# Moving four of twelve weight-sum sets from the recurrence into the output projection

## The chip, the core and the metric

The kernel runs on one core of a Trainium2 chip. A core has a matrix engine (PE, with PEld for its weight loads), three engines for elementwise work (DVE is VectorE, ACT is ScalarE, POOL is GpSimd), a queue engine (SP) that issues transfers, and 16 DMA engines that carry all transfers. Each engine works through its own list of instructions in order and waits on semaphores of the others. The metric is the time of one execution in microseconds (us), lower is better; comparisons are made between medians.

## The reference

Two decoder layers on x of 1024 tokens by 1024 features, all in float32. Layer 0 mixes tokens with a gated linear recurrence (HGRN2), layer 1 with a convolution module. Each mixer is followed by a normalisation with a residual, then a squared-ReLU MLP with a hidden width of 4096, then another normalisation. Cut to what matters here:

```python
for i in range(DEPTH):                                    # two layers
    mix = hgrn2_mixer(x, ...) if i % 2 == 0 else conformer_conv_mixer(x, ...)
    x = layer_norm(DEEPNORM_ALPHA * x + mix, ln_mix_g[i], ln_mix_b[i])
    ff = jnp.square(jax.nn.relu(x @ ffn_w1[i])) @ ffn_w2[i]
    x = layer_norm(DEEPNORM_ALPHA * x + ff, ln_ffn_g[i], ln_ffn_b[i])

def hgrn2_mixer(h, w_in, lb, norm_g, w_out):
    q, fz, v, g = jnp.split(h @ w_in, 4, axis=-1)
    ...                                                   # chunkwise recurrence per head -> o, RMS norm, gate
    return o.astype(h.dtype) @ w_out
```

## The kernel before, in words

Every large product is done by a scheme of seven products in place of eight blocks (the "forms" 1 to 7), each in three passes over high and low halves of float32 numbers. A form of a weight is a block or a sum of blocks. For the second MLP weight, `w2`, the sums are not made on an engine but by the DMA engines, ahead of time: for each of 8 slices `c` of each of the 2 layers there is a **set**, a buffer `sum_w2...` of four 512 KB blocks in DRAM. `block_sums` makes a set with five transfers: two plain copies of two blocks each (L419, L420), one accumulating transfer that adds two blocks at once (L421, 1024 KB), and two accumulating transfers of one block (L423, 512 KB), each of which needs the one ahead of it. Accumulating transfers go out on POOL's queue. The sets are read far later, in the down products of the two MLPs.

Where the 16 sets are made: 12 in the recurrence, with copies and adds on POOL's queue; 2 in the first MLP's up products (L1478, with copies on SP); 2 in layer 1 (L1810). `to_sum` is the list of sets still to make, layer 0 first.

The stages that the change touches, in order of time:

- **The recurrence** (60 to 425 us of the trace). The main loop runs over `PAIRS` and the forms in `ORDER`, 84 products of 12 matmuls (`ps<-xf,fs`). Between the matmuls a hand-written order of ticks (`later`, `tick`) places the work of the 8 heads: the order of all five engines is fixed by the program, with no scheduler. Twice per head `settle` squares the attention output on ACT (L735), POOL makes one over the root (L736 and `power_m_half`, L518), and ACT scales the output by it (L741), for which PE waits with its transposes (`ps<-ident,o`). Every sixth product of the loop, `block_sums` places a set on POOL's queue, its parts 12 ticks apart. A tick fixes only the order on a queue: POOL issues a transfer as soon as it has come to it and the semaphores allow.
- **The output projection** (425 to 509 us). 16 *entries*, one per 128 tokens and half of the columns: 24 matmuls `ps<-w,oT` into one of six PSUM banks, then DVE adds the residual (`y<-y,ps`). At each second half of the columns (entries 3, 4, 6, 7, 9, 11, 13 and 15) follows a norm: statistics on DVE, the power on POOL (L518, `mv<-mv,nhalf`), two DVE passes (`y<-y,mv,ln_mix_g` needs no power, `y<-y,mv,ln_mix_b` does), a store (`kept<-y`), and PE transposes. Here the tile framework's scheduler sets the order of every engine by a simulated timeline.
- **The start of the up products** (from 509 us). `up.form` multiplies the transposed norms by the first forms of `w1q`, which come as `raw` loads on SP (L90, L135) and are split on ACT (L72) and DVE. `x1_late` (L1191) has four small POOL copies there.

Of the kernel before, what the change touches and what calls it, by code (L numbers as in the profile page):

```python
# [8 lines left out]
F32 = mybir.dt.float32  # L9
# [3 lines left out]
ALU = mybir.AluOpType  # L13
PSUM = bass.MemoryType.PSUM

P = 128
# [4 lines left out]
HT = 512  # L21
# [23 lines left out]
ORDER = (1, 2, 6, 5, 7, 3, 4)  # L45
# [66 lines left out]
class Forms(Slots):  # L112
# [12 lines left out]
    def add(self, x, y, out=None):  # L125
        out = self.sums() if out is None else out
        self.vector.tensor_tensor(out=out, in0=x, in1=y, op=ALU.add)
        return out
# [140 lines left out]
def body(ctx, tc, d, out):  # L269
    nc = tc.nc  # L270
    cst = ctx.enter_context(tc.tile_pool(name="cst", bufs=1))
    stat = ctx.enter_context(tc.tile_pool(name="stat", bufs=4))
    dram = ctx.enter_context(tc.tile_pool(name="dram", bufs=1, space=bass.MemoryType.DRAM))
# [55 lines left out]
    def acc():  # L329
        return rings["mm"]()  # L330
# [40 lines left out]
    order = ExitStack()  # L371
# [12 lines left out]
    def later(n, job):  # L384
        if n:
            waiting.append((ticks[0] + n, job))
        else:
            job()

    def tick(n=1):  # L390
        for _ in range(n):
            ticks[0] += 1
            for at, job in [w for w in waiting if w[0] <= ticks[0]]:
                waiting.remove((at, job))
                job()

    sums = {}

    def block_sums(name, layer, c, after=None, gap=0, adds=None):

        t = sums[name, layer, c] = dram.tile([4, P, 1024], F32, name=f"sum_{name}{layer}{c}")
        v, w = t.rearrange("a p n -> p a n"), d[name][layer, c].rearrange("a p n -> p a n")
        queue = nc.sync if after is not None else nc.gpsimd
        if adds is not None:

            def copies(rows, after):
                nc.sync.dma_start(out=t[0:4:2, rows.start, 0:1], in_=after)
                queue.dma_start(out=v[rows, 0:2], in_=w[rows, 0:4:2])
                queue.dma_start(out=v[rows, 2:4], in_=w[rows, 0:2])

            copies(slice(16, P), after)
            adds.append(lambda after: copies(slice(0, 16), after))
            adds.append(lambda after: nc.gpsimd.dma_start(out=v[:, 0:2], in_=w[:, 2:4], accum_op=ALU.add))
            for i in (2, 3):
                adds.append(lambda after, i=i: nc.gpsimd.dma_start(out=v[:, i], in_=v[:, i - 1], accum_op=ALU.add, max_dma_last_dim=4096))
            return
        if after is not None:
            nc.sync.dma_start(out=t[0:4:2, 0, 0:1], in_=after)
        queue.dma_start(out=v[:, 0:2], in_=w[:, 0:4:2])  # L419
        later(gap // 2, lambda: queue.dma_start(out=v[:, 2:4], in_=w[:, 0:2]))  # L420
        parts = [lambda: nc.gpsimd.dma_start(out=v[:, 0:2], in_=w[:, 2:4], accum_op=ALU.add)]  # L421
        for i in (2, 3):
            parts.append(lambda i=i: nc.gpsimd.dma_start(out=v[:, i], in_=v[:, i - 1], accum_op=ALU.add, max_dma_last_dim=4096))  # L423
        for i, part in enumerate(parts):
            later((i + 1) * gap, part)

    to_sum = [(*of, c) for of in (("w2", 0), ("w2", 1)) for c in range(NFC)]

# [72 lines left out]
    for k in range(4):  # L501
        c = slice((k % 2) * HT, (k % 2 + 1) * HT)
# [466 lines left out]
    def seam():  # L969
        plan = [  # L970
            (5, lambda: fetch(0, 0)), (15, lambda: split_w(0, 0, 136)), (17, lambda: split_w(0, 1, 144)), (19, lambda: split_w(0, 3, 120)),
            (21, lambda: split_w(0, 2, 152)), (13, lambda: heads_in(0, 0, 4, 32)), (19, lambda: heads_in(0, 4, 6, 32)),
            (24, lambda: split_heads(0, 0)), (26, lambda: split_heads(0, 2)), (29, lambda: split_heads(0, 4)),
            (16, lambda: bring(0)), (17, lambda: bring(1)), (27, lambda: last_in(H - 2, 0, sixth[0])), (36, lambda: last_in(H - 1, 0, lastly[0])),
            (21, lambda: heads_in(1, 0, 6, 64)), (38, lambda: split_heads(1, 0)), (41, lambda: split_heads(1, 2)), (44, lambda: split_heads(1, 4)),
            (25, lambda: fetch(1, 80)), (39, lambda: split_w(1, 0, 112)), (42, lambda: split_w(1, 1, 128)),
            (45, lambda: split_w(1, 2, 96)), (47, lambda: split_w(1, 3, 104)),
            (43, lambda: last_in(H - 2, 1, sixth[1])), (46, lambda: last_in(H - 1, 1, lastly[1])),
        ]
        for n, job in plan:  # L980
            later(n, job)
# [25 lines left out]
    for p, (kind, j) in enumerate(PAIRS):  # L1007
        st = {"banks": dict(turn_of)}
        turn_of = {"z": turn_of["a"], "a": turn_of["b"], "b": turn_of["z"]}
        pace[1] = 0.0 if p == 0 else 0.6 if p < 3 else 0.5  # L1010
        if kind == "g" and p < len(PAIRS) - 1:
            to_load += [(2 * j, 0), (2 * j + 1, 1), (2 * j, 1), (2 * j + 1, 0)]
        if p == len(PAIRS) - 1:
            seam()
        for i in ORDER:
            if kind == "q" and i == 2:
                while any(a[0] <= j - 3 for a in active) or recs and recs[0] <= j - 3:
                    tick()
                    step()
            pair_product(p, i, made.pop(0), st)  # L1020
            later(2, make_form)
            if (7 * p + ORDER.index(i)) % 6 == 1 and len(to_sum) > 4:
                block_sums(*to_sum.pop(0), gap=12)
        if kind == "q":
            later(4, lambda j=j: recs.append(j))
    early_out = ((0, 0), (1, 0), (2, 0))
# [9 lines left out]
    tick(100)  # L1036
    assert not waiting and not loaded and not to_load and not gates, (waiting, gates)
    order.close()
    oT = [o[0] for o in oT]


# [94 lines left out]
    y = [view(160 + 16 * h, (NTB, D), F32, "y") for h in range(2)][::-1]  # L1136
# [57 lines left out]
    def x1_block(half, t):  # L1194
# [8 lines left out]
        if t < NTB - 1:  # L1203
            bg.chores += [lambda: x1_first(t), lambda: x1_second(t)]

    for half in range(2):
        for t, n in early_out + ((0, 1), (1, 1), (3, 0), (2, 1), (3, 1)) if half == 0 else [(t, n) for t in range(NTB) for n in range(2)]:
            ps = acc()
            if half or (t, n) not in early_out:
                product(ps, wide(oT[half], t, ws[n]))  # L1210
            yv = y[half][:, t, n * HT : (n + 1) * HT]
            vector.scalar_tensor_tensor(out=yv, in0=yv, scalar=ALPHA, in1=ps, op0=ALU.mult, op1=ALU.add)
            if n == 1:
                if half == 1 and t == 0:
                    early[0].ahead(1)
                x1_block(half, t)
                if half == 0 and t:
                    bg.chore()
    for e in early[1:]:
        e.ahead(2)  # L1220


    def store(layer, c, i, q, src):
# [260 lines left out]
    y = [view(32 + 16 * h, (NTB, D), F32, "y") for h in range(2)]  # L1484
# [371 lines left out]
    y = [view(kb, (NTB, D), F32, "y") for kb in (88, 112)]  # L1856
# [103 lines left out]
```

## Time and profile before

| what | us |
|---|---|
| median of 3 runs | 2056.83 (2054.85 to 2059.17) |
| the profiled execution | 2057.16 |
| its span in the trace | 2055.4 |
| PE busy in the span | 2023.6 (98%) |
| PE idle in the span | 31.8 |
| POOL busy in the span | 396.3 (19%) |
| DMA packets of the accumulating and copying queue of POOL (q0) | 12.2% of 16 engines' span |

Times of rows count from the span's start. A row of a timeline gives the start, the duration, the engine, the line, the operation with its tiles, and in brackets how long the engine had been idle before it and what ended that idle time. A row of a waits view gives the total, the number of times and the longest. Line L204 stands for every DVE and PE instruction, since a helper records them; they are told apart by their tiles. `ps` is PSUM. POOL's transfers have a short busy time (the issue); the landing is given apart.

### The profile page before, as it was taken

Reading aid. Unit: us, or ns where it says so; the run is one execution under the profiler, and the core shown is the slowest. Engines: PE = TensorE matmul, PEld = TensorE weight load, DVE = VectorE, ACT = ScalarE, POOL = GpSimd, SP = SyncE. Lnnn points to the kernel's source line nnn. Section 1 sums busy time; section 2 is a strip of 40 time slices with the busy share of each in tenths; the row PEclk is TensorE's granted clock in tenths of the full one; section 3 lists DMA queues with packets and bytes.
Section 4 is the critical chain, followed back from the end, with each engine's and each line's share of the span. In section 5 each row is a group of like instructions: output and inputs, shape, how many; then the busy total and the mean of one; then the engine's idle time right before and its main releaser. Section 6 shows DMA issues by size and latency. Waiting matters only on the chain. (4 is left out here: it accounts for less than half of the span.)

```text
span 2055.4 us, 29649 instructions
## 1 busy us (share of the span) xinstructions
PE 2023.6 (98%) x11144; PEld 1669.0 (81%) x11144; DVE 1488.1 (72%) x1978; ACT 1094.5 (53%) x1725; POOL 396.3 (19%) x405
## 2 busy tenths in 40 slices
PE   8999999999999999999999999999999999999998
PEld 7888887888787888888888888888888878888886
DVE  8698888877856675665567897889589666754456
ACT  5456565631655556444443776498615555443343
POOL 0112232111101000000001798089110000100002
PEclk9999999999999999999999999999999999999999
DMA  4778999842679776989998744496759768995542
GB/s 187 221 201 229 265 254 269 248 183 85 192 268 295 281 282 225 394 329 329 338 335 299 298 185 184 180 351 247 276 216 337 231 225 303 391 292 195 195 154 103
DMA packets 183944, 517.55 MB, mean 252 GB/s; under 512 B 17912, under 2 KB 49784, under 8 KB 182776
## 3 DMA queue, kind: packets, MB, share of 16 engines
q1 hardware_dynamic: 168312, 456.93, 61.7%
q0 software_dynamic: 15488, 58.72, 12.2%
q8 instruction: 87, 1.43, 0.3%
q14 instruction: 57, 0.47, 0.1%
HBM read 380.85 MB, written 201.85 MB: 283 GB/s over the span
## 5 line engine op out<-in xcount | busy, mean ns | idle before, releaser
L204 PE MATMUL ps<-dw,dh 128*128 128x512 f32 x2688 | 611.3, 389 | 0.5 <-DVE dh L204 0.5
L204 PEld LDWEIGHTS ps<-dw,dh 128*128 128x128 f32 x2688 | 504.3, 188 | 105.3 <-DVE dh L204 0.9
L204 PE MATMUL ps<-x1f,fw 128*128 128x512 f32 x1344 | 307.5, 390 | 5.2 <-ACT c L1266 2.3
L204 PEld LDWEIGHTS ps<-x1f,fw 128*128 128x128 f32 x1344 | 251.5, 188 | 59.7 <-issue 2.5
L204 PE MATMUL ps<-xf,fs 128*128 128x512 f32 x1008 | 248.6, 397 | 3.6 <-issue 1.7
L204 POOL TENSOR_TENSOR cb<-cb,prod 128x512 f32<-128x512 f32 x168 | 223.2, 1337 | 13.0 <-ACT prod L1591 2.4
L204 PEld LDWEIGHTS ps<-xf,fs 128*128 128x128 f32 x1008 | 184.0, 188 | 42.6 <-issue 1.9
L204 DVE TENSOR_TENSOR dh<-dh 128x1024 fp32r<-128x1024 f32 x112 | 136.5, 1222 | 109.4 <-ACT dh L72 109.3
L204 DVE SCALAR_TENSOR_TENSOR ps<-u,par,ps 128x512 f32<-128x512 f32 x296 | 206.0, 750 | 10.6 <-ACT ps L1603 9.3
L204 PE MATMUL ps<-xa,wa 128*128 128x512 f32 x864 | 203.3, 392 | 0.2
L72 ACT CAST dh<-dh 128x1024 fp32r<-128x1024 f32 x112 | 117.5, 1051 | 143.9 <-DMA dh<-hf 137.7
L72 ACT CAST dw<-dr 128x1024 fp32r<-128x1024 f32 x112 | 117.4, 1054 | 140.9 <-PE ps L204 125.5
L204 DVE TENSOR_TENSOR dw<-dr,dw 128x1024 fp32r<-128x1024 f32 x112 | 136.3, 1223 | 76.6 <-ACT dw L72 75.8
L204 PEld LDWEIGHTS ps<-xa,wa 128*128 128x128 f32 x864 | 160.3, 188 | 33.6 <-DMA wa<-ready 0.6
L1591 ACT ACTIVATE prod<-u,par 128x512 f32<-128x512 f32 x168 | 119.4, 726 | 34.2 <-POOL cb L204 33.5
L518 POOL TENSOR_TENSOR mv<-mv,nhalf 128x1 f32<-128x1 f32 x32 | 42.2, 1321 | 405.1 <-DVE mv L204 394.8
L204 PE MATMUL ps<-w,oT 128*128 128x512 f32 x384 | 89.9, 392 | 1.3 <-ACT oT L932 0.8
L204 PE MATMUL ps<-xb,wa 128*128 128x512 f32 x384 | 91.1, 393 | 0.0
L204 PE MATMUL ps<-vw,xf 128*128 128x512 f32 x336 | 79.9, 400 | 5.6 <-ACT vw L435 5.3
L204 PEld LDWEIGHTS ps<-w,oT 128*128 128x128 f32 x384 | 71.4, 188 | 16.6 <-ACT oT L932 1.2
L204 PEld LDWEIGHTS ps<-xb,wa 128*128 128x128 f32 x384 | 71.1, 188 | 14.3
L204 PEld LDWEIGHTS ps<-vw,xf 128*128 128x128 f32 x336 | 65.0, 194 | 20.1 <-ACT vw L435 5.3
(250 smaller groups left out, 2891.9 us busy)
## 6 DMA issues: line engine op xcount, KB each, us to landing
wa<-ready SPq DMA_DIRECT2D x140, 512.0 KB, 5.0
dh<-hf SPq DMA_DIRECT2D x112, 512.0 KB, 5.3
sum_w<-in_w_dram POOLq DMA_DIRECT2D x40, 1024.0 KB, 10.0
ready<-spare SPq DMA_DIRECT2D x76, 512.0 KB, 5.7
raw<-in_w1q_dram SPq DMA_DIRECT2D x66, 512.0 KB, 4.3
dr<-sum_w SPq DMA_DIRECT2D x64, 512.0 KB, 5.5
hf<-ht SPq DMA_DIRECT2D x112, 256.0 KB, 4.9
dr<-in_w_dram SPq DMA_DIRECT2D x48, 512.0 KB, 5.3
```

What stands on the lines that cost most here:

```text
L72: self.nc.scalar.copy(out=slot[:, 0, c], in_=raw[:, c])
L204: return op(*args, **kw)
L518: nc.gpsimd.tensor_tensor(out=dst, in0=src, in1=nhalf[:, :n], op=ALU.pow)
L1591: nc.scalar.activation(tp, u[:, k : k + HT], AF.Copy, scale=tap(j, k))
```

## The change

In the recurrence 8 sets are made in place of 12, one every ninth product, their parts 18 ticks apart. Four sets (of layer 1) move to the output projection. There, POOL's order is now written by hand, and no longer chosen by the scheduler: a table `turns` says behind which entry which part of which of the four sets is placed, so that each add stands on POOL's queue behind the power of that entry's norm. The two copies of these sets go out on SP, behind a small transfer of four numbers of `y` into the set's buffer, which holds them back until that entry's `y` is there. The sets in the first MLP and in layer 1 stay as they are.

```diff
@@ new helper @@
+    def sum_parts(name, layer, c):
+        t = sums[name, layer, c] = dram.tile([4, P, 1024], F32, name=f"sum_{name}{layer}{c}")
+        v, w = t.rearrange("a p n -> p a n"), d[name][layer, c].rearrange("a p n -> p a n")
+
+        def copies(after):
+            nc.sync.dma_start(out=t[0:4:2, 0, 0:1], in_=after)
+            nc.sync.dma_start(out=v[:, 0:2], in_=w[:, 0:4:2])
+            nc.sync.dma_start(out=v[:, 2:4], in_=w[:, 0:2])
+
+        def add(out, x, **kw):
+            return lambda after: nc.gpsimd.dma_start(out=out, in_=x, accum_op=ALU.add, **kw)
+
+        return [copies, add(v[:, 0:2], w[:, 2:4])] + [add(v[:, i], v[:, i - 1], max_dma_last_dim=4096) for i in (2, 3)]
@@ recurrence @@
-            if (7 * p + ORDER.index(i)) % 6 == 1 and len(to_sum) > 4:
-                block_sums(*to_sum.pop(0), gap=12)
+            if (7 * p + ORDER.index(i)) % 9 == 1 and len(to_sum) > 8:
+                block_sums(*to_sum.pop(0), gap=18)
...
     order.close()
+    order.enter_context(tc.manual_schedule(engines={mybir.EngineType.Pool}))
@@ output projection @@
+    parts, entry = [sum_parts(*to_sum.pop(0)) for _ in range(4)], 0
+    turns = {0: (0,), 3: (1,), 4: (0,), 6: (0, 1, 2), 8: (3,), 9: (0, 1, 2), 11: (1, 2, 3), 13: (2, 3), 15: (3,)}
     for half in range(2):
...
+            for k in turns.get(entry, ()):
+                parts[k].pop(0)(y[half][:2, t, n * HT : n * HT + 1])
+            entry += 1
+    assert not any(parts)
     for e in early[1:]:
         e.ahead(2)
+    order.close()
```

How the lists of instructions move, at the three places that the prediction speaks of. POOL's list around the two `settle` steps of the fourth head in the recurrence (`ss<-ss` is the mean, `ss<-ss,nhalf` the power; `sum_w` with a number is one set), before:

```order
L419 DMA sum_w_2457<-in_w_dram 128x2x1024
L420 DMA sum_w_2457<-in_w_dram 128x2x1024
L736 TENSOR_SCALAR ss<-ss 128x4
L518 TENSOR_TENSOR ss<-ss,nhalf 128x4
L423 DMA sum_w_2229<-sum_w_2229 128x1024
L421 DMA sum_w_2457<-in_w_dram 128x2x1024
L736 TENSOR_SCALAR ss<-ss 128x4
L518 TENSOR_TENSOR ss<-ss,nhalf 128x4
L423 DMA sum_w_2457<-sum_w_2457 128x1024
```

and with the change, at the same two steps:

```order
L420 DMA sum_w_2217<-in_w_dram 128x2x1024
L423 DMA sum_w_1816<-sum_w_1816 128x1024
L421 DMA sum_w_2217<-in_w_dram 128x2x1024
L751 TENSOR_SCALAR ss<-ss 128x4
L533 TENSOR_TENSOR ss<-ss,nhalf 128x4
L423 DMA sum_w_2217<-sum_w_2217 128x1024
L419 DMA sum_w_2541<-in_w_dram 128x2x1024
L751 TENSOR_SCALAR ss<-ss 128x4
L533 TENSOR_TENSOR ss<-ss,nhalf 128x4
L420 DMA sum_w_2541<-in_w_dram 128x2x1024
```

Between the two steps stood an add that needs two copies just issued (L421); now there stand the add of an older transfer and a copy that needs nothing.

POOL's list in the output projection had the eight powers in one row, with the copies of `x1_late` behind them:

```order
L736 TENSOR_SCALAR ss<-ss 128x4
L518 TENSOR_TENSOR ss<-ss,nhalf 128x4
L518 TENSOR_TENSOR mv<-mv,nhalf 128x1 x8
L1191 CAST x1f_4506<-fw 128x1 x2
L1191 CAST x1f_4510<-fw 128x1 x2
```

and has with the change, from the third power to the last but one (the sets are 4491 to 4494):

```order
L533 TENSOR_TENSOR mv<-mv,nhalf 128x1
L438 DMA sum_w_4491<-sum_w_4491 128x1024
L438 DMA sum_w_4492<-in_w_dram 128x2x1024
L533 TENSOR_TENSOR mv<-mv,nhalf 128x1 x2
L438 DMA sum_w_4491<-sum_w_4491 128x1024
L438 DMA sum_w_4492<-sum_w_4492 128x1024
L438 DMA sum_w_4493<-in_w_dram 128x2x1024
L533 TENSOR_TENSOR mv<-mv,nhalf 128x1
L438 DMA sum_w_4492<-sum_w_4492 128x1024
L438 DMA sum_w_4493<-sum_w_4493 128x1024
L438 DMA sum_w_4494<-in_w_dram 128x2x1024
L533 TENSOR_TENSOR mv<-mv,nhalf 128x1
```

Twelve adds now stand between and behind the powers; each waits on POOL's queue for the copy or add that it needs, with the next power behind it.

POOL's list around the two settles of the sixth head, before:

```order
L419 DMA sum_w_3242<-in_w_dram 128x2x1024
L420 DMA sum_w_3242<-in_w_dram 128x2x1024
L423 DMA sum_w_2921<-sum_w_2921 128x1024
L421 DMA sum_w_3242<-in_w_dram 128x2x1024
L736 TENSOR_SCALAR ss<-ss 128x4
L518 TENSOR_TENSOR ss<-ss,nhalf 128x4
L736 TENSOR_SCALAR ss<-ss 128x4
L518 TENSOR_TENSOR ss<-ss,nhalf 128x4
L423 DMA sum_w_3242<-sum_w_3242 128x1024
```

and with the change:

```order
L421 DMA sum_w_2903<-in_w_dram 128x2x1024
L423 DMA sum_w_2903<-sum_w_2903 128x1024
L419 DMA sum_w_3307<-in_w_dram 128x2x1024
L751 TENSOR_SCALAR ss<-ss 128x4
L533 TENSOR_TENSOR ss<-ss,nhalf 128x4
L420 DMA sum_w_3307<-in_w_dram 128x2x1024
L751 TENSOR_SCALAR ss<-ss 128x4
L533 TENSOR_TENSOR ss<-ss,nhalf 128x4
L423 DMA sum_w_2903<-sum_w_2903 128x1024
```

One copy stands ahead of the first settle there now, in place of two copies and two adds, and one between the two.

On SP's list in the output projection the small transfer and the two copies of a set stand behind the gain vectors' load (first set), the first, the third and the fourth store `kept<-y`; of the weight loads of the up products one stands between the third set's small transfer and its copies, and all others behind the fourth set's copies. The scheduler also moved a few DVE instructions of entries 8 to 11 past each other.

## The prediction

> **What bounds the kernel now.** First the page's busy times and the busy time by stage (stage, then busy time and count of each engine, granted clock, share of the DMA engines, GB/s):
>
> ```profile
> PE 2023.6 (98%) x11144; PEld 1669.0 (81%) x11144; DVE 1488.1 (72%) x1978; ACT 1094.5 (53%) x1725; POOL 396.3 (19%) x405
> 60.00:425.00 365.00, 356.18 (x3677) 294.44 (x3676) 293.67 (x471) 219.27 (x502) 79.42 (x94) 1.00 0.90 252
> 425.00:509.00 84.00, 84.00 (x398) 69.99 (x397) 64.34 (x95) 14.31 (x22) 10.44 (x7) 1.00 0.24 84
> 509.00:560.00 51.00, 47.69 (x214) 38.30 (x213) 46.18 (x54) 30.93 (x43) 8.66 (x9) 1.00 0.61 185
> ```
>
> PE sets the time: it idles 31.8 us in all. The recurrence (60 to 425) holds 365 - 356.18 = 8.8 of them, the output projection (425 to 509) none, the start of the up products 3.3. The DMA engines are 90% taken in the recurrence and 24% in the projection, and the change carries work from the one to the other. It can win at most the 8.8 us in which PE waits, so I read next what PE waits for there, and who made that late (total, times, longest):
>
> ```profile
> PE ps L204 <- issue: 1.7, 1, 1.7
> PE ps L204 <- DVE state L204: 1.4, 2, 0.9
> PE ps L204 <- ACT t L837: 1.2, 2, 0.9
> PE ps L204 <- ACT o L741: 1.1, 2, 0.7
> ...
> PE ps L204 <- DMA f<-vd: 0.2, 1, 0.2
> ```
>
> Only 0.2 us is a transfer directly. The others wait for ACT or DVE, so I followed the stalls back through the timelines. Two go back to the sets. At 268 POOL is late (POOL, ACT and PE in one stretch):
>
> ```profile
> 262.26 0.23 ACT L735 ACTIVATION_READ_ACCUMULATOR o<-ps 128x1 f32 x1
> 263.26 1.22 POOL L421 DMA_DIRECT2D sum_w<-in_w_dram  x1 [3.68 <-issue]
> 264.56 0.72 POOL L736 TENSOR_SCALAR ss<-ss 128x4 f32<-128x4 f32 x1
> 266.76 1.15 ACT L741 ACTIVATE o<-ps,ss 128x128 f32<-128x128 f32 x4 [1.94 <-POOL ss L518]
> 267.96 0.66 PE L204 MATMUL ps<-ident,o 128*128 128x128 f32 x4 [0.71 <-ACT o L741]
> ```
>
> ACT had its sums at 262.49. POOL stood until 263.26 at the add L421, which needs two copies just issued, and began the mean at 264.56: 2.07 us late, of which PE loses 0.71. At 343 ACT is late, since a store has not landed and its buffer isn't free:
>
> ```profile
> 342.37 0.59 ACT L837 COPY t<-ps 128x512 f32<-128x512 f32 x1 [1.72 <-DMA zd<-t]
> 343.00 2.09 PE L204 MATMUL ps<-xf,fs 128*128 128x512 f32 x8 [0.31 <-ACT t L837]
> 346.81 1.09 PE L204 MATMUL ps<-xf,fs 128*128 128x512 f32 x4 [1.71 <-issue]
> ```
>
> ACT loses 1.72, and PE 0.31 + 1.71 = 2.02 behind it. The other 8.8 - 0.71 - 2.02 - 0.2 = 5.9 us stand behind DVE and ACT, which work there without a transfer in sight: DVE is busy 293.67 of 365 us.
>
> **The change, part by part.** The load first (the recurrence's queues and transfers; KB each, then the median us to landing):
>
> ```profile
> q0 software_dynamic: 13248, 50.34, 56.6%
> sum_w<-in_w_dram POOLq DMA_DIRECT2D x36, 1024.0 KB, 10.0
> sum_w<-sum_w POOLq DMA_DIRECT2D x24, 512.0 KB, 7.1
> ```
>
> POOL's queue takes 0.566 x 365 = 207 us of all 16 engines for 12 sets, 17 us a set. Four sets less leave 365 x 0.90 - 69 = 260 us, a share of 0.71.
>
> *Recurrence, the wait at 268.* In the new order of POOL nothing that was just issued stands between the two settles of a head, only an add whose source has been in flight since before the first settle, and a copy. Gain 0.71; none, if another settle is caught instead. I take 0.7.
>
> *Recurrence, the wait at 343.* It lies at the sixth head's settles. Ahead of them POOL had issued a copy pair, a small add and a large add; now it has one copy there, behind an add whose source is long in flight, so the store has less beside it. Gain between 0 and 2.0; I take 1.5, nearer the whole, since ACT needs only 1.72 us less. The 5.9 us behind DVE and ACT stay: no instruction of theirs goes. The 20 issues of four sets leave POOL's list, which was not the bound.
>
> *Projection, POOL.* Here adds stand ahead of powers. The rows that tell what a late power costs:
>
> ```profile
> 452.85 1.28 DVE L204 SCALAR_TENSOR_TENSOR y<-y,mv,ln_mix_b 128x1024 f32<-128x1024 f32 x1 [0.45 <-POOL mv L518]
> 463.62 1.51 POOL L518 TENSOR_TENSOR mv<-mv,nhalf 128x1 f32<-128x1 f32 x1 [4.82 <-DVE mv L204]
> 465.17 1.29 DVE L204 SCALAR_TENSOR_TENSOR y<-y,mv,ln_mix_b 128x1024 f32<-128x1024 f32 x1 [0.44 <-POOL mv L518]
> 473.62 1.29 DVE L204 TENSOR_TENSOR x1f<-ps,x1f 128x512 fp32r<-128x512 f32 x2 [3.50 <-ACT x1f L1045]
> 491.04 1.45 POOL L518 TENSOR_TENSOR mv<-mv,nhalf 128x1 f32<-128x1 f32 x1 [12.78 <-DVE mv L204]
> 497.06 0.69 DVE L204 SCALAR_TENSOR_TENSOR y<-y,ps 128x512 f32<-128x512 f32 x1 [2.58 <-PE ps L204]
> 499.05 1.45 POOL L518 TENSOR_TENSOR mv<-mv,nhalf 128x1 f32<-128x1 f32 x1 [6.57 <-DVE mv L204]
> 510.83 1.45 POOL L518 TENSOR_TENSOR mv<-mv,nhalf 128x1 f32<-128x1 f32 x1 [10.33 <-DMA raw<-in_w1q_dram]
> 513.53 1.28 DVE L204 SCALAR_TENSOR_TENSOR y<-y,mv,ln_mix_b 128x1024 f32<-128x1024 f32 x1
> ```
>
> I step through the new list with these times, 10 us for a large add, 7.1 for a small one, and 1.2 and 0.9 us to issue them (the rows at 263.26 and 93.39). The first add goes out behind entry 4's power, which ends where DVE goes on, at 452.85, and lands at 462.8; only then does the second go, then the other set's first, so entry 7's power starts at about 465, not 463.62. DVE has it 1 to 3 us late (3 if the add takes 12). Behind it DVE idles 3.50 us before 473.62: that covers it, and what it would cost without that is the same 1 to 3 us. Behind the powers of entries 9 and 11 (the latter at 491.04) go three adds each. The last of the three at 491 starts at 494.1 and must land before the last one behind entry 13's power (499.05) can go: 504.1, with entry 15's power due at 510.83, over 6 us later. So POOL costs nothing up to a landing time of about 14 us: 16 us would bring that add to 510.1, but by then the earlier ones hold each other up too.
>
> That three adds in one go hold this is bounded by the same load on this queue in the recurrence, an add of 512 KB and two copies of 1024 KB issued within 2 us:
>
> ```profile
> 93.39 0.87 POOL L423 DMA_DIRECT2D sum_w<-sum_w  x1 [12.12 <-DMA sum_w<-in_w_dram]
> 94.68 1.02 POOL L420 DMA_DIRECT2D sum_w<-in_w_dram  x1
> 106.08 1.20 POOL L421 DMA_DIRECT2D sum_w<-in_w_dram  x1 [5.05 <-issue]
> ```
>
> 2.5 MB had landed 12.7 us after the first issue; three adds are 2 MB. Under 14, so I take 0, with the end up to 8 us (rival 2).
>
> *Projection, SP.* Each pair of copies waits for its small transfer, and the stores behind it wait with them; nobody reads those stores before the first MLP's end. The one weight load in that stretch stands ahead of the third pair. Copies: 4 x 2 MB in a stage where the DMA engines are 76% free. Nothing.
>
> *Start of the up products, loads.* DVE is busy 46.18 of the 51 us there, and PE waits behind it:
>
> ```profile
> 506.43 1.06 ACT L72 CAST fw<-raw 128x1024 fp32r<-128x1024 f32 x1 [1.99 <-DMA raw<-in_w1q_dram]
> 507.60 1.22 DVE L204 TENSOR_TENSOR fw<-raw,fw 128x1024 fp32r<-128x1024 f32 x1
> 511.17 1.05 ACT L72 CAST fw<-raw 128x1024 fp32r<-128x1024 f32 x1 [3.68 <-DMA raw<-in_w1q_dram]
> 534.90 11.56 PE L204 MATMUL ps<-x1f,fw 128*128 128x512 f32 x48 [1.47 <-ACT fw L72]
> raw<-in_w1q_dram SPq DMA_DIRECT2D x15, 512.0 KB, 4.5
> raw<-in_wout_dram SPq DMA_DIRECT2D x8, 512.0 KB, 8.3
> ```
>
> DVE takes the weight at 507.60, right when ACT is done with it (507.49): whatever the load is late, DVE is late, and PE at 534.90. The last three small adds now run beside these loads. Lower bound 0 (4.5 us, as now), upper bound 8.3 - 4.5 = 3.8 (the same size in a crowd of loads). I take 1.0, near the lower end, since one small add at a time is no crowd.
>
> Sum: -0.7 - 1.5 + 1.0 = -1.2 us on the profiled execution's 2057.16, so 2056.0. The median of the runs is 2056.83, 0.3 lower: **2055.6**.
>
> **The rivals.** *1, the relief is worth more.* If the waits behind ACT and DVE are knock-ons of late transfers, two thirds of the 8.8 go: -5.9 with nothing given back, 2050.9. For it: DMA share 0.90. Against it: the waits that I followed back to DVE have it working without a gap.
>
> *2, POOL's queue holds the last norms.* Point: landing beyond 14 us. At 16 us for a large add and 13 for a small one, the same stepping starts the three adds behind entry 11's power at 498.5 to 503.3 in place of 492.4 to 494.1; entry 13's power then ends 5.4 us after the 500.5 at which DVE needs it, and entry 15's another 2.8 late, both where DVE has next to no gap: 8.2 - 2.2 = +6.0, 2062.8, slower. For it: adds come in threes, beside copies and weight loads. Against it: the 12.7 us above.
>
> *3, loads land only behind the adds.* The store at 343 hints at a load's end tied to others'. Then the weight of 506.43 comes with the add issued at 494.1, at 504 to 506, in time; the one of 511.17 comes with the small add issued at 504 to 507, 7.1 later: up to 514.1, +2.9. Net 2.9 - 2.2 = +0.7, 2057.5. [...]
>
> **How the numbers follow.** Forecast 0.60 (its own range 2053 to 2058), rival 1 0.21, rival 2 0.11, rival 3 0.08. A change within 0.2% (4.1 us, 2052.7 to 2060.9) can't be told from none here. Faster by more: most of rival 1 and a tail of the forecast, 0.24. Slower by more: rival 2 and a little of 3, 0.13. The rest, 0.63, is no change. The range of eight in ten takes in rival 1's middle and stops short of rival 2's: 2050.5 to 2060.5.
>
> **What would show it.** Right: DMA share near 0.7 in the recurrence; no idle of ACT before L741 as long as 1.9; PE idle there of 6 to 7 us; entry 7's power at 465 or later with PE still without idle in the projection; PE idle of 3 to 5 us after it. Wrong: recurrence idle unchanged or under 4 (rival 1); the powers of entries 13 and 15 later than DVE needs them (rival 2); the casts of 506.43 and 511.17 over 2 us later against PE's end of the projection (rival 3).

## The result and the profile after

The changed kernel takes 2065.1 us (median of 22 runs, 2062.15 to 2071.69), the kernel before 2057.23 (22 runs, 2053.30 to 2066.86). The ratio is 1.0035, with a 95% interval of 1.0027 to 1.0043: 7.2 us slower by the ratio, 7.9 by the medians. The forecast was 2055.6 with a range of 2050.5 to 2060.5, so the result lies outside the range, on the other side of no change. The profiled execution's span is 2064.0 us, against 2055.4 before: 8.6 us more.

First the busy time by stage, in the columns of the prediction (stage, length, then busy time and count of PE, PEld, DVE, ACT and POOL, granted clock, DMA share, GB/s). The kernel before, in two stages cut a little differently than in the prediction:

```profile
425.00:512.00 87.00, 87.00 (x413) 72.50 (x412) 67.24 (x100) 15.14 (x23) 11.61 (x8) 1.00 0.26 92
512.00:580.00 68.00, 64.69 (x286) 52.34 (x285) 54.68 (x63) 40.23 (x58) 8.49 (x11) 1.00 0.71 217
```

The changed kernel:

```profile
PE 2027.4 (98%) x11144; PEld 1671.3 (81%) x11144; DVE 1488.1 (72%) x1978; ACT 1092.6 (53%) x1725; POOL 385.9 (19%) x397
60.00:425.00 365.00, 354.64 (x3672) 293.49 (x3671) 292.88 (x470) 217.71 (x501) 60.64 (x74) 1.00 0.72 205
425.00:512.00 87.00, 84.86 (x398) 70.17 (x397) 59.20 (x86) 13.03 (x21) 16.80 (x16) 1.00 0.87 246
512.00:580.00 68.00, 60.18 (x248) 47.13 (x247) 56.32 (x68) 38.55 (x55) 12.15 (x13) 0.92 0.77 211
460.00:480.00 20.00, 20.00 (x101) 16.52 (x100) 13.07 (x20) 4.37 (x7) 4.04 (x6) 1.00 1.02 273
480.00:500.00 20.00, 17.86 (x83) 14.54 (x83) 13.66 (x20) 1.73 (x3) 4.49 (x5) 1.00 1.04 261
500.00:520.00 20.00, 19.17 (x93) 15.41 (x91) 13.24 (x22) 2.68 (x4) 3.48 (x5) 1.00 1.05 242
520.00:540.00 20.00, 14.99 (x57) 11.42 (x56) 12.78 (x17) 7.11 (x11) 2.32 (x3) 0.83 0.75 218
```

Three things show here. The recurrence's DMA share fell as forecast, 0.90 to 0.72 (0.71 expected), but PE does not idle less there: 10.4 us in place of 8.8. The projection and what follows have no room left: from 460 to 520 the 16 DMA engines are busy all the time (as the view counts packets, a little over 1). And PE, which never idled in the projection, now idles 2.1 us there and 7.8 after it, and is granted 0.83 of its clock from 520 to 540.

The 8.6 us of span are 4.8 of PE's idle time (31.8 to 36.6) and 3.8 of PE's busy time (2023.6 to 2027.4) with the same 11144 matmuls. The longer busy time stands in one group (busy us, mean ns of one), first before, then after:

```profile
L204 PE MATMUL ps<-x1f,fw 128*128 128x512 f32 x1344 | 307.5, 390 | 5.2 <-ACT c L1266 2.3 <-ACT fw L72 1.5 <-DVE c L204 1.4
```

```profile
L204 PE MATMUL ps<-x1f,fw 128*128 128x512 f32 x1344 | 311.9, 394 | 7.5 <-ACT fw L72 6.5 <-DVE c L204 0.8 <-ACT c L1289 0.2
```

What the transfers of 425 to 530 cost in the changed kernel (queue: packets, MB, share of 16 engines; issue: count, KB each, median us to landing):

```profile
q1 hardware_dynamic: 4964, 18.49, 49.6%
q0 software_dynamic: 2096, 7.87, 40.3%
sum_w<-in_w_dram POOLq DMA_DIRECT2D x4, 1024.0 KB, 14.7
sum_w<-sum_w POOLq DMA_DIRECT2D x8, 512.0 KB, 9.7
raw<-in_w1q_dram SPq DMA_DIRECT2D x8, 512.0 KB, 7.0
```

A large add lands after 14.7 us (10.0 in the recurrence before), a weight load after 7.0 (4.4 before in the same stretch). The queues' shares give the price of a byte: q1 took 0.496 x 105 = 52.1 us of all 16 engines for 18.49 MB, 2.8 us per MB; the adds on q0 took 42.3 us for 7.87 MB, 5.4 us per MB, twice as much.

Now the chain of events, from the timelines (POOL, SP, DVE, PE and ACT, in order of time; the lines stand 15 to 23 further down in the file than before; L533 is the power, L438 an add, L433 and L434 the gate and the first copy):

```profile
454.09 1.25 POOL L438 DMA_DIRECT2D sum_w<-in_w_dram  x1
468.16 0.88 POOL L438 DMA_DIRECT2D sum_w<-sum_w  x1 [8.02 <-DMA sum_w<-in_w_dram]
469.52 1.31 POOL L533 TENSOR_TENSOR mv<-mv,nhalf 128x1 f32<-128x1 f32 x1
470.86 1.28 DVE L204 SCALAR_TENSOR_TENSOR y<-y,mv,ln_mix_b 128x1024 f32<-128x1024 f32 x1 [4.81 <-POOL mv L533]
473.97 0.25 SPq L433 DMA_DIRECT2D sum_w<-y  x1
485.73 0.56 SPq L434 DMA_DIRECT2D sum_w<-in_w_dram  x1
485.74 1.28 DVE L204 SCALAR_TENSOR_TENSOR y<-y,mv,ln_mix_g 128x1024 f32<-128x1024 f32 x1 [7.11 <-DMA sum_w<-y]
488.48 0.65 PE L204 MATMUL ps<-ident,y 128*128 128x128 f32 x4 [2.14 <-DVE y L204]
505.16 0.82 POOL L438 DMA_DIRECT2D sum_w<-sum_w  x1 [6.73 <-DMA sum_w<-in_w_dram]
509.00 1.04 POOL L533 TENSOR_TENSOR mv<-mv,nhalf 128x1 f32<-128x1 f32 x1
510.08 1.28 DVE L204 SCALAR_TENSOR_TENSOR y<-y,mv,ln_mix_b 128x1024 f32<-128x1024 f32 x1 [5.45 <-POOL mv L533]
523.64 1.04 ACT L72 CAST fw<-raw 128x1024 fp32r<-128x1024 f32 x1 [8.78 <-DMA raw<-in_w1q_dram]
524.74 1.51 PE L204 MATMUL ps<-x1f,fw 128*128 128x512 f32 x4 [4.40 <-ACT fw L72]
```

Three waits are new. POOL stands before an add whose source lands late, and the power behind that add keeps DVE waiting: 4.81 us for entry 7's norm, 5.45 for entry 13's. The gate of the fourth set, a transfer of four numbers, takes 11.8 us (473.97 to 485.73), and DVE waits 7.11 for it, since the norm of entry 9 overwrites in place the `y` that the gate still reads. And the first weights of the up products come late: ACT waits 8.78 for a load and PE 4.40 behind it. That load left SP later and was longer on its way (before, then after; SP's rows):

```profile
507.47 0.81 SPq L90 DMA_DIRECT2D raw<-in_w1q_dram  x2
```

```profile
511.39 0.32 SPq L1121 DMA_DIRECT2D kept<-y  x1
511.80 0.88 SPq L90 DMA_DIRECT2D raw<-in_w1q_dram  x2
```

From issue to cast it took 511.17 - 507.47 = 3.7 us before and 523.64 - 511.80 = 11.8 in the change. The cast is 12.5 us later: 4.3 of that is the later issue, right behind a store for which SP had waited on entry 13's late norm, and 8.1 is the longer way.

### The profile page after: what moved, and what is told of

It reads as the page before. It is cut to its first block, busy times and chain, and to the rows that moved or that the text cites. A ratio compares the mean times of both kernels' runs of the same rounds, so it can differ in the third digit from the quotient of the medians.

```text
span 2064.0 us, 29659 instructions
## 1 busy us (share of the span) xinstructions
PE 2027.4 (98%) x11144; PEld 1671.3 (81%) x11144; DVE 1488.1 (72%) x1978; ACT 1092.6 (53%) x1725; POOL 385.9 (19%) x397
## 5 line engine op out<-in xcount | busy, mean ns | idle before, releaser
L204 PE MATMUL ps<-x1f,fw 128*128 128x512 f32 x1344 | 311.9, 394 | 7.5 <-ACT fw L72 6.5
L204 DVE SCALAR_TENSOR_TENSOR ps<-u,par,ps 128x512 f32<-128x512 f32 x296 | 205.9, 750 | 10.4 <-ACT ps L1626 9.1
L533 POOL TENSOR_TENSOR mv<-mv,nhalf 128x1 f32<-128x1 f32 x32 | 40.2, 1257 | 369.5 <-DVE mv L204 369.5
```

The costliest lines, as they stand in the source:

```text
L204: return op(*args, **kw)
L533: nc.gpsimd.tensor_tensor(out=dst, in0=src, in1=nhalf[:, :n], op=ALU.pow)
```

## The experiments

Two theories stood after the two traces. **Share**: the transfers of four sets do not fit into the projection, and all three waits are one cause. **Order**: a part of the change does the harm by its place alone, POOL's list written by hand, or the gate that reads `y`. PE's idle time by stage, its busy time and the DMA shares of all profiles stand together here (worked out from the views of windows: length of the stage less PE's busy time in it); the sections below refer to them. Each row's profile is of one execution. Those of the gate at entry 7 and of the adds that need nothing took 2071.2 and 2069.4 us, over 4 us more than the medians of their kernels, so their idle times are high.

| kernel | median us | ratio to before (95%) | PE idle 60:425 | 425:512 | 512:580 | PE busy, span | DMA share 460:500 | 500:525 |
|---|---|---|---|---|---|---|---|---|
| before | 2057.2 to 2057.9 | 1 | 8.8 | 0 | 3.3 | 2023.6 | 0.17 | 0.51 |
| the change | 2065.10 | 1.0035 [1.0027, 1.0043] | 10.4 | 2.1 | 7.8 | 2027.4 | 1.03 | 1.05 |
| no sets in the projection | 2052.69 | 0.9983 [0.9972, 0.9994] | 8.4 | 0 | 2.0 | 2022.9 | 0.17 | 0.48 |
| gate at entry 7 | 2066.94 | 1.0049 [1.0033, 1.0065] | 10.1 | 0.5 | 11.3 | 2029.9 | 1.02 | 1.03 |
| all adds small | 2053.58 | 0.9979 [0.9969, 0.9989] | 8.4 | 0 | 2.0 | 2024.2 | 0.62 | 0.56 |
| adds that need nothing | 2064.17 | 1.0033 [1.0019, 1.0047] | 8.2 | 2.6 | 9.8 | 2027.0 | 1.03 | 1.03 |
| adds alone, no copies | 2060.61 | 1.0014 [1.0004, 1.0025] | 9.6 | 0 | 7.6 | 2025.0 | 0.84 | 1.02 |
| first six adds small | 2056.85 | 0.9999 [0.9988, 1.0010] | 9.1 | 0 | 5.4 | 2027.0 | 0.70 | 1.01 |
| last six adds small | 2055.12 | 0.9985 [0.9974, 0.9997] | 8.2 | 2.1 | 3.3 | 2022.2 | 1.02 | 0.72 |
| 9 sets and 3 | 2053.72 | 0.9986 [0.9975, 0.9998] | 7.7 | 0 | 4.1 | 2021.7 | 0.90 | 0.85 |
| 10 sets and 2 | 2052.13 | 0.9974 [0.9965, 0.9983] | 6.3 | 0 | 3.3 | 2022.1 | 0.65 | 0.62 |
| 11 sets and 1 | 2054.80 | 0.9982 [0.9970, 0.9993] | 7.9 | 0 | 3.3 | 2023.2 | 0.50 | 0.50 |

**Without the four sets.** The recurrence of the change, but nothing in the projection; the down products of layer 1 read plain blocks for those sets.

```diff
-    parts, entry = [sum_parts(*to_sum.pop(0)) for _ in range(4)], 0
-    turns = {0: (0,), 3: (1,), 4: (0,), 6: (0, 1, 2), 8: (3,), ...}
+    left_out = {to_sum.pop(0) for _ in range(4)}
+    parts, entry, turns = [], 0, {}
```

> Left out: the four sets of the output projection are not made at all (the down product of layer 1 reads plain blocks of w2 in their place, as many and as large), so only the thinning of the recurrence from 12 to 8 sets is left. If all of the loss sits in the projection (the share theory: 4 sets x 17 us of DMA time do not fit into an 84 us stage that already uses 20), the time is that of before or 1 to 3 us under it (2054 to 2057 beside a before of 2057), with no idle of PE in the projection and 3 us behind it. If the thinned recurrence itself loses (its PE idle was 10.4 us in the changed kernel against 8.8), it stays 1 to 3 us above before.

Measured 2052.69, ratio 0.9983: some 4 us under before and 11 to 12 under the change. So the four sets in the projection cost 11 to 12 us, and the loss is theirs, not the recurrence's.

**The same orders, little load.** Every add covers 16 of 128 rows; all issues, places and the full copies stay. Under the share theory the loss goes; under the order theory the powers of entries 7 and 13 stay late, and a part of the loss with them.

```diff
+        h = slice(0, 16)
-        return [copies, add(v[:, 0:2], w[:, 2:4])] + [add(v[:, i], v[:, i - 1], ...) for i in (2, 3)]
+        return [copies, add(v[h, 0:2], w[h, 2:4])] + [add(v[h, i], v[h, i - 1], ...) for i in (2, 3)]
```

> Left out: 112 of 128 rows of the twelve adds in the projection (16 rows are added); order, waits and number of instructions stay as in the changed kernel, the bytes of the adds fall to an eighth. Share theory: with 7 MB less in the stage the adds land in under 8 us, no power is late, the gate transfer lands in 2 to 3 us, and the loss is gone (within 2 us of before, 2055 to 2059). [...]

Measured 2053.58, ratio 0.9979. POOL's timeline in the same places as above:

```profile
452.78 0.88 POOL L438 DMA_DIRECT2D sum_w<-in_w_dram  x1
463.63 1.53 POOL L534 TENSOR_TENSOR mv<-mv,nhalf 128x1 f32<-128x1 f32 x1 [1.59 <-DVE mv L204]
499.06 1.46 POOL L534 TENSOR_TENSOR mv<-mv,nhalf 128x1 f32<-128x1 f32 x1 [4.13 <-DVE mv L204]
```

Entry 7's power starts at 463.63 (before 463.62) and entry 13's at 499.06 (before 499.05). The list written by hand, the gates and the full copies are all still there, and cost nothing that can be measured. That rules out order as the sole cause: the loss needs the load of the adds.

**The gate one entry earlier**, where no norm overwrites what it reads before it is done:

```diff
-    turns = {..., 6: (0, 1, 2), 8: (3,), 9: (0, 1, 2), ...}
+    turns = {..., 6: (0, 1, 2), 7: (3,), 9: (0, 1, 2), ...}
```

> One entry of the table is moved: the copies of the fourth set stand behind entry 7 in place of entry 8, so that their small gate transfer reads y of a norm that is already finished. In the changed kernel DVE stood 7.1 us at entry 9 until that gate transfer had read the y that the norm overwrites in place. Gate theory: this wait is most of the loss, 5 of the 7 us come back (2058 to 2060 beside a before of 2057). Share theory: the wait goes, but the adds and loads behind it stay as late as they are, so at most 2 us come back (2062 to 2065) and the powers of entries 13 and 15 and the weight loads are late as in the changed kernel.

Measured 2066.94, ratio 1.0049. The wait for the gate is gone from DVE's waits (total, times, longest, in 425 to 560), but those for the powers have grown from 11.6 us, and a wait for a store is new. The two come to 19.2 us, where the powers and the gate took 18.7 in the change:

```profile
DVE y L204 <- POOL mv L533: 15.9, 6, 8.8
DVE xl L204 <- DMA kept<-y: 3.3, 1, 3.3
```

The copies start earlier and, as I read it, take the engines from the adds. The gate is where some of the time shows; taking it away returned nothing.

**Adds that need no copy and no other add**: they go into sets of layer 0 that are finished by then, from inputs, with the same bytes; so the sums of neither layer are the reference's, and no add needs what another transfer brings.

```diff
-        return [copies, add(v[:, 0:2], w[:, 2:4])] + [add(v[:, i], v[:, i - 1], ...) for i in (2, 3)]
+        u = sums[name, 0, c].rearrange("a p n -> p a n")
+        return [copies, add(u[:, 0:2], w[:, 2:4])] + [add(u[:, i], w[:, i], ...) for i in (2, 3)]
```

> Changed in what is computed: the twelve adds of the projection go into finished sets of layer 0, each with a source in the inputs, so that none of them waits for a copy or for another add; bytes, number and places on POOL's list stay, the four moved sets are left as bare copies. If POOL's queue is the way in which the loss comes about (powers behind waiting adds), the powers are on time and most of the 7 us come back (2058 to 2060 beside a before of 2057). If it is the share of the DMA engines that counts, the adds crowd in earlier, the gate transfer and the weight loads are as late as before or later, and the time stays at 2062 to 2066.

Measured 2064.17, ratio 1.0033, where the change has 1.0035 and the intervals overlap. DVE's waits stay too, and POOL still stands before adds:

```profile
DVE y L204 <- POOL mv L534: 10.9, 5, 4.9
DVE y L204 <- DMA sum_w<-y: 7.4, 1, 7.4
468.07 1.17 POOL L438 DMA_DIRECT2D sum_w<-in_w_dram  x1 [8.19 <-issue]
468.81 1.02 POOL L534 TENSOR_TENSOR mv<-mv,nhalf 128x1 f32<-128x1 f32 x1
```

I had read POOL's delay as a chain of adds that need each other. That need is not what it takes: without it the powers are as late, at the same DMA shares. But this kernel did not free POOL's queue. POOL stood 28.5 us before six adds, with nothing that the profile shows to wait for, and went on 7.8 to 15.1 us after the issue of the add two ahead (the row at 468.07 comes 15.1 us after that of 453.00), while a large add landed after 13.8 us and a small one after 11.4 (medians of 425 to 512). So the run does not tell a full queue of POOL from full DMA engines; the next one does so in part.

**The adds alone**, as in the kernel just told, without copies and gates (the down products of layer 1 read plain blocks):

```diff
         def copies(after):
-            nc.sync.dma_start(out=t[0:4:2, 0, 0:1], in_=after)
-            nc.sync.dma_start(out=v[:, 0:2], in_=w[:, 0:4:2])
-            nc.sync.dma_start(out=v[:, 2:4], in_=w[:, 0:2])
+            pass
```

> The four projection sets have their twelve full adds on POOL's queue in the change's places, into finished sets from inputs as in the kernel whose adds wait for nothing, but no copies and no gate transfers on SP; the down products of layer 1 read plain blocks for these sets, so the output is not the reference's. Share theory: the load is the projection's own 20 us plus the adds' 35, 55 of 84, so adds land in about 10 us, the powers are on time, the weights of the up products too: 2053 to 2057. Rival (accumulating transfers of full size hold up POOL's queue whatever runs beside them): powers of entries 7 and 13 as late as with the copies (468, 507), 2061 to 2065.

Measured 2060.61, ratio 1.0014: neither range. The powers are on time, DVE never waits over 0.5 us for one, as the share theory has it, though POOL stood 17.9 us before five adds in the same way: the adds land sooner (10.0 us for a large one). But PE still has a gap of 4.23 us at the first weights. The price of an add is clean here, since q0 carries nothing else (425 to 530):

```profile
q0 software_dynamic: 2240, 8.39, 44.5%
521.22 10.32 PE L204 MATMUL ps<-x1f,fw 128*128 128x512 f32 x36 [4.23 <-ACT fw L72]
```

0.445 x 105 = 46.7 us for 8.39 MB, 5.6 us per MB. My figure for the whole stage (55 us of 84) hid where the load lies: 0.84 from 460 to 500, but 1.02 from 500 to 525, where the weights of the up products are loaded.

**Which half of the adds.** Two kernels, each with six of the twelve adds over 16 rows: the last six in the one, the first six in the other.

```diff
+        small = {(1, 2), (2, 1), (2, 2), (3, 0), (3, 1), (3, 2)}   # last six
+        small = {(0, 0), (0, 1), (0, 2), (1, 0), (1, 1), (2, 0)}   # first six, in the other kernel
+        h = [slice(0, 16) if (k, j) in small else slice(0, P) for j in range(3)]
```

> The change, with the last six of the twelve adds (from the one behind entry 9's first add on: all three of the fourth set, the last two of the third, the last of the second) over 16 of 128 rows, so the sums of layer 1 are incomplete there. At 5.6 us of all DMA engines per MB of adds (46.7 us for 8.4 MB in the kernel that had adds alone) this takes 17 us of load from 490 to 540 and nothing ahead of it. Theory (the loss has two parts: late norms in the projection, 3.5 us of delay, and late weight loads with the lower PE clock behind them, about 8.7, of which some is won back later): the late power of entry 7 and the wait at the gate stay, the weights are on time, no PE gap of 4 us, no stretch at a lower clock; 2055 to 2058. Rival (the late norms make the loads late too, since SP and the buffers follow them): the gap stays, 2061 to 2065.

> The complement: the first six adds over 16 of 128 rows (the first set, the first two of the second, the first of the third), the last six whole, so the sums of layer 1 are incomplete there. This takes 22 us of load from 453 to 495. Theory: entry 7's power and the gate are on time, the projection runs without PE idle, but from 491 six adds of 3.5 MB (20 us) stand beside the weight loads, so the weights are late by some us, with a PE gap of 2 to 4; 2056 to 2061. Rival (the loss begins with the first late norm): all on time, 2052 to 2055.

With the last six small, 2055.12 and 0.9985. Entry 7's norm and the wait at the gate are as late as in the change, entry 13's norm in part (DVE waits 3.01 us for its power in place of 5.45), and PE hardly notices:

```profile
469.34 1.28 DVE L204 SCALAR_TENSOR_TENSOR y<-y,mv,ln_mix_b 128x1024 f32<-128x1024 f32 x1 [5.37 <-POOL mv L535]
483.70 1.28 DVE L204 SCALAR_TENSOR_TENSOR y<-y,mv,ln_mix_g 128x1024 f32<-128x1024 f32 x1 [6.60 <-DMA sum_w<-y]
486.44 0.66 PE L204 MATMUL ps<-ident,y 128*128 128x128 f32 x4 [1.65 <-DVE y L204]
500.00:520.00 20.00, 20.00 (x98) 16.64 (x97) 16.71 (x25) 5.86 (x8) 6.03 (x7) 1.00 0.70 201
```

With the first six small, 2056.85 and 0.9999. No norm is late, but the first weights are:

```profile
500.00:520.00 20.00, 16.60 (x81) 13.49 (x79) 13.48 (x21) 3.82 (x5) 5.92 (x6) 0.97 1.01 267
520.04 11.09 PE L204 MATMUL ps<-x1f,fw 128*128 128x512 f32 x36 [3.44 <-ACT fw L72]
```

Against the kernel with all adds small (2053.58) the first half of the load costs 1.5 us, the second 3.3, and both 11.5. By the ratios it is 1.2, 4.1 and 11.5. The noise of such a difference is some 3 us either way, so the first half alone does not stand clear of it and the second just does. What the two cost together beyond their sum is 6.2 us, give or take 4. One step of it shows at the weights' load that went out at 511.80 in the change. Its cast came at 511.17 before, at 518.94 with the first six small, at 513.67 with the last six small and at 523.64 in the change: 7.8, 2.5 and 12.5 us late, more with both halves than the 10.3 of the two together. In the change it is both held up behind the late norm's store and slow on its way. The adds move too. In the change the last one is issued at 528.75 and the DMA engines are full until 530; with the first six small it goes out at 519.09, and the share falls from 1.01 (520 to 525) to 0.49 (525 to 530). So the late half is pushed further into the weight loads. How much each step is worth, the runs do not show.

**How many sets fit.** Three mixes of the same kind, all with the full sums:

```diff
-            if (7 * p + ORDER.index(i)) % 9 == 1 and len(to_sum) > 8:
-                block_sums(*to_sum.pop(0), gap=18)
+            if (7 * p + ORDER.index(i)) % 7 == 1 and len(to_sum) > 6:      # 10 and 2
+                block_sums(*to_sum.pop(0), gap=14)
...
+    turns = {0: (0,), 3: (1,), 6: (0,), 9: (0, 1), 11: (0, 1), 13: (1,)}  # 10 and 2
+    turns = {0: (0,), 3: (1,), 4: (0,), 6: (0, 1, 2), 9: (0, 1), 11: (1, 2), 13: (2,), 15: (2,)}  # 9 and 3
+    turns = {0: (0,), 6: (0,), 9: (0,), 11: (0,)}  # 11 and 1
```

> Ten sets in the recurrence (every seventh product, parts 14 ticks apart), two in the projection, in the same way as the change's four. Share theory (the transfers of four sets don't fit into the projection): the load is the projection's own 20 us plus 2 x 17 = 54 of 84 us, so the adds land in 10 us, the powers of entries 9, 11 and 13 are on time, PE has no idle in the projection, and the start of the up products is as in the kernel before; the time is that of the kernel before less up to half of what the recurrence gains with eight sets: 2054 to 2057. Order theory (hand-written POOL order or the gate transfers hurt by themselves): half of the change's loss stays, 2060 to 2062.

> Nine sets in the recurrence (every eighth product, parts 16 ticks apart), three in the projection. Share theory: 20 + 3 x 17 = 71 of 84 us on the mean, but most of it between entries 6 and 15, so the DMA share there comes near 1, one power is late, and the time lies between the two neighbours: 2056 to 2061. If the loss goes in proportion to the number of sets: three quarters of the change's, 2061 to 2063.

> Eleven sets in the recurrence (every seventh product, parts 14 ticks apart), one in the projection (gate at entry 0, adds behind the powers of entries 6, 9 and 11). If the gain of the kernel with ten and two comes from the spacing in the recurrence and the lower load there in proportion: 2053 to 2055. If it needs the DMA share there well under 0.9: about 2055 to 2057.

Measured 2052.13 with two sets (2 us under the range given), 2053.72 with three, 2054.80 with one. By number of sets in the projection, 0, 1, 2, 3, 4: 2052.7 (without their work), 2054.8, 2052.1, 2053.7, 2065.1. Up to three cost next to nothing, and the fourth 10 to 11 us; the places of the adds and the number of sets in the recurrence differ too. Neither of my two expectations for three sets was right: it is no slope but an edge, between shares of 0.90 and 0.85 in the two stretches of the table (three sets) and 1.03 and 1.05 (four). A share of 1 in one stretch alone cost less: 1.5 us and 3.3 above, 7.0 with the adds alone, against all adds small. With three, one power is 4.8 us late and the store of a norm holds DVE for 4.2, but PE has no idle time in the projection. The kernel with ten and two beats both: 0.9974 (0.9965 to 0.9983), 5 us under before and 13 under the change. Its stages:

```profile
60.00:425.00 365.00, 358.73 (x3692) 297.18 (x3691) 296.92 (x475) 222.54 (x506) 69.45 (x84) 1.00 0.82 232
425.00:512.00 87.00, 87.00 (x413) 72.15 (x412) 65.79 (x98) 13.58 (x21) 17.73 (x14) 1.00 0.67 183
```

**The kernel before a second time**, to see which of its small stalls belong to it.

> The kernel before, profiled a second time. If PE's stalls of 1.9 us at 657 to 664 and of about 2 us at 1650 to 1690 belong to the kernel, they return; if they are the chance of one execution, they are gone, and the span is some 2 to 4 us shorter than 2055.4, near 2052.

One execution of 2056.57, span 2054.8. Both stalls that I had asked for return: 1.5 us of PE's idle time from 580 to 700 (1.9 in the first profile) and 2.2 from 1630 to 1710 (2.0). In the eleven other kernels the second is 0.0 to 0.4, whatever the load, the kernel with one set in the projection too. So about 2 us of each gain or loss here come from a place far behind the change, where before's DVE takes a weight (`sum<-raw`) just too late. Why any form of the change removes it, no run tells. What hardly returned is the wait on which I had put the larger gain; ACT's waits of 60 to 425, first profile, then second:

```profile
ACT o L741 <- POOL ss L518: 4.5, 5, 1.9
ACT t L837 <- DMA zd<-t: 1.7, 1, 1.7
```

```profile
ACT o L741 <- POOL ss L518: 11.3, 8, 2.9
ACT t L837 <- DMA zd<-t: 0.3, 1, 0.3
```

## Why the prediction was wrong

**The step that failed** is "Copies: 4 x 2 MB in a stage where the DMA engines are 76% free. Nothing." The prediction had worked out 17 us of all 16 engines for a set, used it to take 69 us out of the recurrence, and got that stage's new share right (0.71, measured 0.72). It never put the same 69 us into the stage that receives them: 84 x 0.24 = 20 us of its own and 69 more are 89 in 84. That is what the runs show: from 425 to 530 the two queues took 52.1 + 42.3 = 94.4 us of all engines, where the kernel before took 28.5 (q1, 27.1%), so the sets brought 66, with one add still to go. The sum follows from two rows that were quoted, and says that the stage is full with four sets and not with three (72); the runs put the edge in the same place. The copies were priced by the stage's share before, the adds by landing times of the recurrence, and each alone would have fitted.

**Landing times.** "Under 14, so I take 0" rested on 2.5 MB that had landed after 12.7 us. There the share was 0.90 on the mean; here it is 1.03 from 460 to 500, and the large adds take 14.7, the small ones 9.7. The comparison also went by bytes: at the prices found here the 0.5 MB add and two copies are some 9 us of all engines, and three adds of 2 MB some 11. The first add went out at 454.09 and the next, which needs it, could go only at 468.16, so entry 7's power started at 469.52 and not at "about 465". The cover that I named for it, DVE's 3.50 us before 473.62, was less than the 4.81.

**The gate and SP's list.** I followed which stores wait behind the gate on SP, and missed who waits for what it reads: DVE's norm overwrites `y` in place. With all adds small the wait at the gate costs DVE nothing, at a full share 7.11 us. I also missed that weight loads stand on SP behind the norms' stores, so that a late norm makes a load late (511.39 and 511.80).

**The rivals.** Rival 2 named the mechanism that begins the loss and even its size, entry 13's power 5.4 us late (DVE waited 5.45), and its 2062.8 was the nearest of the four numbers. That the 5.4 fits is in part luck, since it was stepped with landings of 16 and 13 us where 14.7 and 9.7 were measured. And its price is not what PE pays: with the late norms but no late weights it was 1.5 us (last six adds small), since PE has work of other entries. Rival 3's place is where PE's longest gap lies, and its 2.9 us are near the 3.3 that late loads alone cost (first six small); given the noise of both, that too may be luck. That loads land only behind the adds, on which its 2.9 rests, no run shows: measured is a load that was cast 11.8 us after its issue, at DMA shares of 1.03 and 1.05 (515 to 525), which plain sharing of full engines could give as well. What neither had is that the two meet, 11.5 us in place of 4.8, and that PE's clock falls behind the gap (to 0.54 from 525 to 530 in the change).

**The start of the up products**: 1.0 us was taken, between 0 and 3.8. Measured: PE's idle time from 512 to 580 went from 3.3 to 7.8, and with the matmuls of 307.5 us that became 311.9 the step was too small by some 8 us.

**The recurrence.** The two waits at 268 and 343 are gone, as forecast: ACT's longest wait for POOL fell from 1.9 to 1.0 and `zd<-t` no longer holds it. PE did not gain from it, 8.8 to 10.4 us, since other late transfers came in their place (PE's waits there, in the changed kernel; the first goes back to a load, for which DVE's `total<-pr` waits 1.95 us at 210):

```profile
PE ps L204 <- ACT kt L739: 2.4, 1, 2.4
PE ps L204 <- DMA f<-vd: 2.2, 1, 2.2
```

With eight sets in the recurrence PE idles 8.2 to 10.4 us in eight profiles, before 8.8 and 9.3 in two: no gain that stands out. In before's second profile ACT waits 0.27 us for `zd<-t`, and PE's 1.71 in the same place is still 1.07, so a good part of that stall was not ACT's lateness. A single stall of under 2 us in one profile of such a stage is too little to price; what is left of a gain in the recurrence shows with ten sets (6.3), in one profile.

## What to carry to other kernels

When work is moved from one stage to another, put its price into the receiving stage with the same measure with which it is taken out of the giving one, and compare the sum with the stage's length: for transfers this is the time of all DMA engines, not a landing time. Do it in stretches of some 20 us, since a stage that has room on the mean can be full where the next stage's first loads fall. Up to a share of about 0.9 (three sets: 0.90 and 0.85) the order of the transfers mattered little here; with 1 from 460 to 525 (1.03 and 1.05) every wait in the stage grew at once, and taking away the gate, or the adds' need of each other, returned nothing. And when an experiment is to remove a wait, look in its trace whether the wait is gone: in the second of these POOL still stood before its adds.

## What the runs showed of the hardware

**A slower PE after a gap.** In the five kernels with a PE gap of more than 3 us between the projection and the up products (3.44, 4.00, 4.23, 4.40 and 6.08), the granted clock was lower behind the gap. In steps of 5 us it was 0.50 to 0.73 in the lowest (0.54 in the change, 525 to 530) and 0.77 to 1.00 in the one after that (0.77 in the change). In the change 520 to 540 shows 0.83, and the group of `ps<-x1f,fw` took 4.4 us more for the same 1344 matmuls. Before, and with one, two or three sets, where no gap in that stretch is over 1.48, the clock from 512 to 580 is 1.00. But a long gap is not all that goes with a lower clock. In two profiles, the kernel without the sets and the one with all adds small, the clock from 512 to 580 is 0.97, with no gap over 1.48 us. And the change has a second spell (540 to 560 shows 0.91), behind a gap as long as before's:

```profile
548.46 12.80 PE L204 MATMUL ps<-x1f,fw 128*128 128x512 f32 x48 [1.47 <-ACT fw L72]
```

The same 48 matmuls took 11.56 us before, at 534.90, behind 1.47 us too. So 1.2 of the 4.4 us do not belong to the long gap. The kernels with the gate at entry 7 and with the first six adds small show this second spell as well (12.80 and 12.79).

**The price of an accumulating transfer** between buffers in DRAM is 5.4 to 5.6 us of all 16 engines per MB, twice the 2.8 of the queue that carries copies, loads and stores. A set (2.1 MB of copies and 2.1 MB of adds) is so some 17 us, and two thirds of that are its adds.

**A queue that holds.** In the kernel whose adds need nothing and in the one with the adds alone POOL stood 28.5 and 17.9 us before full-size adds, eleven times, with nothing that the profile shows to wait for. The change has two such stops, 1.50 us before the add at 488.97 and 2.28 before that at 508.26; both ended 0.3 us after the add two ahead had landed (issued at 479.27 and 497.53, landed 9.4 and 10.4 us later). So, as far as the profile shows, it was not enough there that POOL had come to a transfer and its semaphores allowed it. With adds of 16 rows there is no such stop. What sets the limit, no run tells; a power behind such an add waits with it.

**A tiny transfer at a full share.** The gate moves four numbers and took 11.8 us. The copies behind the four gates of the change went out 1.1, 2.3, 5.7 and 11.8 us after them, in order of time, at DMA shares of 0.00, 0.58, 1.05 and 1.05 meanwhile. With all adds small (share 0.62 from 460 to 500) DVE's waits show none for a gate. So a transfer of next to no size on SP's queue took longer here when the DMA engines were full with what POOL's queue and SP's own had put there.
